# A decoder layer on one core: the split down weights of the first FFN go through DRAM between its two passes

## The chip, the cores and the metric

The kernel runs on one core of one Trainium2 chip. The metric is the time of one execution in microseconds (us) of device time; the median of three runs before the change is 1908.28 us.

## What is computed

One decoder layer over 1040 positions (16 meta tokens and 1024 inputs) of width 1024, in float32. Cut to what matters here:

```
h_res = h_res + 0.5 * swiglu_ffn(rmsnorm(h_res), w_gate, w_up, w_down)     # FFN 1, hidden width 2816
proj  = rmsnorm(h_res) @ w_in
h_res = h_res + concat([diff_attention(q, k, v), conformer_conv(u)]) @ w_out
h_res = h_res + 0.5 * swiglu_ffn(rmsnorm(h_res), w_gate2, w_up2, w_down2)  # FFN 2
y     = rmsnorm(h_res)[:, 16:]

swiglu_ffn(x, g, u, d) = (silu(x @ g) * (x @ u)) @ d
```

The down weights of FFN 1 are a 2816 x 1024 matrix; they are needed for every position.

## The kernel before

The positions are worked on in two halves, of 528 (the meta tokens with them) and of 512. So each FFN has two passes and reads all its weights twice. The hidden width is 22 blocks `f` of 128, in chunks of 4, 4, 4, 2, 4 and 4 blocks (`CHUNKS`). In a chunk TensorE first makes the gate and up products of its blocks (tiles `pg` and `pu`, or `p` where two blocks are made together by a scheme with seven products, class `Pairs`), VectorE and ScalarE turn them into the hidden activations `h`, and TensorE then makes the down products (`dn`): four weight tiles per chunk, each for two of the eight output blocks. VectorE adds each `dn` to the residual `x` (L241). Ahead of the down products of a chunk the next block or pair is already made (`pend`), except around the last chunk.

Products are made in fp32r, a reduced format, three times: each operand is split in a high part (`x` rounded) and a low part (the rest), and high by high, high by low and low by high are summed. Weights are split on the chip by `load_w` (L107 on): SyncE (SP) issues a load of 512 KB into a tile `wraw` (two slots), ScalarE (ACT) rounds it into the first half of a tile `whl` (L128), and VectorE (DVE) subtracts to make the second half (L129). `whl` has four slots, one rotation for all weights; a slot is free again when TensorE has read its tile to the end. `Pairs` has raw tiles of its own (`raw`) beside `wraw`. Each engine works through its instructions in program order, and so does the DMA queue of SP; that order is set by a scheduler, in which loads and splits of weights rank 500 places ahead (`AHEAD`).

In the second pass of FFN 1 the attention and the convolution of the first half run beside the FFN: attention scores `sc`, transposes `tm` and values `o` sit between the products of TensorE, and the 31-tap convolution (`acc`, L556) on VectorE. Both passes use the same down weights: in the first pass `ffn` is called with `FB[0]` (two blocks of 264 columns), in the second with `FB[1]` (one block of 512). GpSimd (POOL) issues only stores: `kscr`, `qscr`, `vscr` (keys, queries, values), `acscr`, `xscr` (the residual after a pass) and some small ones.

Of the kernel before, what the change touches and what calls it, by code (L numbers as in the profile page):

```python
# [9 lines left out]
F32 = mybir.dt.float32  # L10
F32R = mybir.dt.float32r
# [7 lines left out]
P = 128  # L19
# [7 lines left out]
CHUNKS = [4, 4, 4, 2, 4, 4]  # L27
PLAIN = 4
# [4 lines left out]
AHEAD = 500  # L33
# [7 lines left out]
FB = [[(0, HM // 2), (HM // 2, HM // 2)], [(0, HB)]]  # L41
# [10 lines left out]
def layer(ctx, tc, xb, wgu1, wd1, win, wv, wo, wgu2, wd2, colv, lamv, consts, cossin, out):  # L52
    nc = tc.nc
    V, S, T = nc.vector, nc.scalar, nc.tensor
    dma = nc.sync.dma_start
    store = nc.gpsimd.dma_start

    def mm(o, lhsT, rhs, start, stop):
        T.matmul(o, lhsT, rhs, start=start, stop=stop)  # L59

    def pool(stack, name, bufs, side="left"):
        return stack.enter_context(tc.tile_pool(name=name, bufs=bufs, side=side, reuse_waits="tile"))
# [3 lines left out]
    wph = pool(ctx, "whl", 4)  # L66
# [7 lines left out]
    dram = ctx.enter_context(tc.tile_pool(name="dscr", bufs=1, space=DRAM))  # L74
# [4 lines left out]
    xscr = dram.tile([2, P, ND, HB], F32, tag="xscr", name="xscr")  # L79
    rtok = dram.tile([2, HM], F32, tag="rtok", name="rtok")  # L80
    rscr = dram.tile([2, 4, HB], F32, tag="rscr", name="rscr")
    acscr = dram.tile([2, 8, P, 2, HB], F32, tag="acscr", name="acscr")

    rA = const.tile([P, HM], F32, tag="rA", name="rA")
# [13 lines left out]
    def col(i):  # L98
        return cols[:, i:i + 1]

    def psg(name):
        return psG.tile([P, 512], F32, tag="g", name=name)
# [4 lines left out]
    def load_w(src, n=1024, rp=None):  # L107
        with tc.high_priority(offset=AHEAD):
            raw = (rp or wpr).tile([P, 1024], F32, tag="wraw", name="wraw")
            dma(raw[:, :n], src)  # L110
            hl = wph.tile([P, 2, 1024], F32R, tag="whl", name="whl")
            split(hl[:, 0, :n], hl[:, 1, :n], raw[:, :n])
        return hl

    first = []
# [11 lines left out]
    def split(dst_hi, dst_lo, src):  # L127
        S.copy(dst_hi, src)  # L128
        return V.tensor_tensor(dst_lo, src, dst_hi.bitcast(F32), op=ALU.subtract)  # L129
# [43 lines left out]
    def tiles(hl, o=0, n=ND):  # L173
        return [hl[:, :, o + k * P:o + (k + 1) * P] for k in range(n)]
# [8 lines left out]
    def proj_pair(pss, hls, c0, w):  # L183
        for n, (a, xx) in enumerate(((0, xh), (1, xh), (0, xl))):
            for ps, hl in zip(pss, hls):
                for k in range(ND):
                    mm(ps, hl[:, a, k * P:(k + 1) * P], xx[:, k, c0:c0 + w], n == 0 and k == 0, n == 2 and k == ND - 1)

    def ffn(blocks, last_blocks, wgu, wd, x, after, step, before_last, start=False, scaled=False, flat=0, pair_of=None, ahead=None):
        def gate_up(f):  # L190
            if start and f < 2:
                hg, hu = first[2 * f:2 * f + 2]
            else:
                hg, hu = load_w(wgu[f, 0]), load_w(wgu[f, 1])
            if f >= flat:
                wsg, wsu = [tiles(hg, o, 4) + tiles(hu, o, 4) for o in (0, 512)]
            else:
                wsg, wsu = tiles(hg), tiles(hu)
            h = hp.tile([P, 2, HM], F32R, tag="h", name="h")
            for c0, w in blocks:  # L200
                pair = start and f == 0
                if pair:
                    if c0 == 0:
                        pg, pu = psg("pg")[:, :w], psg("pu")[:, :w]
                    else:
                        both = psS.tile([P, 2, 512], F32, tag="s", name="both")
                        pg, pu = both[:, 0, :w], both[:, 1, :w]
                    proj_pair((pg, pu), (hg, hu), c0, w)
                else:
                    pg = psg("pg")[:, :w]  # L210
                    proj(pg, wsg, c0, w)
                rb = rA[:, c0:c0 + w]
                tw = tmp.tile([P, 512], F32, tag="e", name="t")[:, :w]
                th = tmp.tile([P, 512], F32, tag="th", name="th")[:, :w]
                if scaled:
                    S.activation(th, pg, AF.Tanh, scale=0.5)
                    last[0] = V.scalar_tensor_tensor(tw, th, 1.0, pg, op0=ALU.add, op1=ALU.mult)  # L217
                else:
                    V.tensor_tensor(tw, pg, rb, op=ALU.mult)
                    S.activation(th, tw, AF.Tanh, scale=0.5)  # L220
                    V.tensor_tensor(tw, tw, rb, op=ALU.mult)
                    last[0] = V.scalar_tensor_tensor(tw, th, 1.0, tw, op0=ALU.add, op1=ALU.mult)
                step()
                if not pair:
                    pu = psg("pu")[:, :w]
                    proj(pu, wsu, c0, w)
                V.tensor_tensor(tw, pu, tw, op=ALU.mult)
                last[0] = split(h[:, 0, c0:c0 + w], h[:, 1, c0:c0 + w], tw)
            step()
            return [[h]]  # L230

        def down_piece(hl, n, j, d, hs, c0, w):
            m = psg("dn")
            for f in range(n):
                o = (j * n + f) * P
                wh, wl = hl[:, 0, o:o + P], hl[:, 1, o:o + P]
                mm(m[:, :w], wh, hs[f][0][:, 0, c0:c0 + w], f == 0, False)
                mm(m[:, :w], wh, hs[f][0][:, 1, c0:c0 + w], False, False)
                mm(m[:, :w], wl, hs[f][0][:, 0, c0:c0 + w], False, f == n - 1)
            xs = x[:, d, c0:c0 + w]  # L240
            last[0] = V.scalar_tensor_tensor(xs, m[:, :w], 0.25, xs, op0=ALU.mult, op1=ALU.add)  # L241

        def make(f):
            return pair_of(f) if pair_of and f >= flat else gate_up(f)

        offs = 0
        f = 0
        pend = []
        for ci, n in enumerate(CHUNKS):
            hs = pend  # L250
            final = ci == len(CHUNKS) - 1
            if final and ahead is not None:
                ahead()
            while len(hs) < n:
                new = make(f)
                f += len(new)
                hs = hs + new
            pend = []
            if final:
                if pair_of:  # L260
                    pair_of.flush()
                before_last()
            elif not (pair_of and f == flat):
                pend = make(f)
                f += len(pend)
            srcs = []
            for dp in range(4):
                sz = P * 2 * n * P
                srcs.append(wd[offs:offs + sz].rearrange("(p c) -> p c", p=P))
                offs += sz  # L270
            if not final:
                for dp in range(4):
                    hl = load_w(srcs[dp], 2 * n * P)
                    for j in range(2):
                        for c0, w in blocks:
                            down_piece(hl, n, j, 2 * dp + j, hs, c0, w)
                    step()
            else:
                hls = [load_w(s, 2 * n * P) for s in srcs]
                for c0, w in last_blocks:  # L280
                    for d in range(ND):
                        down_piece(hls[d // 2], n, d % 2, d, hs, c0, w)
                        after(c0, w, d)
# [63 lines left out]
    def mix_in(b, x):  # L347
        sums = {}

        def f(c0, w, d):  # L350
            if d == 0:
                sums[c0] = tmp.tile([P, 512], F32, tag="ssum", name="ssum")
            xs = x[:, d, c0:c0 + w]
            gain_piece(xs, col(C_GM + d), xh[:, d, c0:c0 + w], xl[:, d, c0:c0 + w])
            sq_piece(xs, w, sums[c0], d == 0)
            if d == ND - 1:
                norm_r(rB[:, c0:c0 + w], w, sums[c0], 95 if c0 + w == FB[b][-1][0] + FB[b][-1][1] else 60)
                a = max(c0, RO[b])
                store(xscr[b][:, :, a - RO[b]:c0 + w - RO[b]], x[:, :, a:c0 + w])
        return f  # L360
# [588 lines left out]
    x = ffn1_first()  # L949
# [4 lines left out]
    first_pairs = Pairs(wgu1, H2, {}, True)  # L954
# [46 lines left out]
        first_pairs.e = pool(es_s, "e1", 2, side="right")  # L1001

    first_pairs.ready.append(first_ready)
    ffn(FB[0], FB[0], wgu1, wd1, x, mix_in(0, x), first_step, setup_consts, start=True, flat=PLAIN, pair_of=first_pairs)
    es_s.close()
    es_z = ExitStack()
    zp.append(pool(es_z, "zp", 5, side="right"))
# [9 lines left out]
    x = res.pop()  # L1017
# [3 lines left out]
    bg = mixer(mid_pools(es_m, 0), zs)  # L1021
# [3 lines left out]
            pass  # L1025

    next(bg, None)
    ffn(FB[1], FB[1], wgu1, wd1, x, mix_in(1, x), lambda: next(bg, None), drain, scaled=True, flat=PLAIN)
    es_m.close()
    zs = []  # L1030
    es_l = ExitStack()
# [14 lines left out]
    x = res.pop()  # L1046
# [4 lines left out]
    bg = mixer(mid_pools(es_m, 1), zs)  # L1051
# [182 lines left out]
```

## Time and profile before

| what | value |
|---|---|
| median of 3 runs | 1908.28 us (1907.56 to 1909.43) |
| the profiled execution, its own time | 1906.57 us |
| its span, first to last instruction | 1904.8 us |
| TensorE busy, matmuls | 1883.7 us (99%) |
| TensorE weight loads (PEld) | 1673.5 us (88%) |
| VectorE busy | 1486.7 us (78%) |
| ScalarE busy | 828.5 us (43%) |
| read from HBM, written | 215.72 MB, 31.61 MB |

The profiled execution is one of the program, 1.71 us below the median of the three runs; 1.77 us of its time lie outside its span. In the span the first pass of FFN 1 has its down products and pairs from about 58 to 372 us, the input projection follows up to 497 us, and the second pass runs from 497 to 905 us. Shares of busy time are means over stages; which engine is waited for in a stage is read from the waits.

### The profile page before, as it was taken

How to read it: one execution, taken by the hardware profiler on the slowest of the kernel's cores; microseconds unless marked ns; L12 is line 12 of the kernel's file. 1: busy time of each engine (PE TensorE's matmuls, PEld its weight loads, DVE VectorE, ACT ScalarE, POOL GpSimd, SP SyncE). 2: the span in 40 equal slices, each digit the busy share in tenths (PEclk: the TensorE clock that was granted, in tenths of full speed). 3: DMA queues.
4: the chain of work that ended last, by engine and by line, in shares of the span. 5: the costliest groups of instructions: out<-in, count | busy, mean ns of one | idle time of the engine just before them, and what ended most of it. 6: DMA issues, size and time to landing. Idle time of an engine off the chain costs nothing.

```text
span 1904.8 us, 29083 instructions
## 1 busy us (share of the span) xinstructions
PE 1883.7 (99%) x11542; PEld 1673.5 (88%) x11542; DVE 1486.7 (78%) x2317; ACT 828.5 (43%) x1407; POOL 70.1 (4%) x132
## 2 busy tenths in 40 slices
PE   9999999999999999999999999999999999999997
PEld 9999999999888888778878888888879889999997
DVE  8997787867687877866558788888785898977877
ACT  6453444532333333534223354444453455434434
POOL 0000000003100000020001100000021000000000
PEclk9999999999999999999999999999999999999999
DMA  5232332445633333273535733424258533323322
GB/s 183 80 115 84 95 95 99 136 156 166 192 101 110 122 100 101 89 253 115 206 100 155 222 107 105 144 89 120 90 191 297 166 122 123 134 98 106 101 93 67
DMA packets 89000, 249.22 MB, mean 131 GB/s; under 512 B 10928, under 2 KB 26032, under 8 KB 88608
## 3 DMA queue, kind: packets, MB, share of 16 engines
q1 hardware_dynamic: 79888, 217.85, 35.6%
q0 software_dynamic: 8976, 29.52, 4.7%
q8 instruction: 90, 1.47, 0.3%
q14 instruction: 46, 0.38, 0.1%
HBM read 215.72 MB, written 31.61 MB: 130 GB/s over the span
## 4 chain that ended last, share of the span: by engine, by line
PE 89%; DVE 6%; DMA 2%; ACT 2%; issue 1%; SPq 0%; DVEq 0%; ACTq 0%
PE dn L59 24%; PE p L874 20%; PE pg L59 15%; PE pu L59 12%; PE pa L59 5%; PE pv L59 3%; PE pb L59 2%; PE wo L59 2%; PE sc L59 2%; DVE whl L129 2%; PE o L59 1%; ACT whl L128 1%; PE tm L482 1%; PE v L59 1%; DMA wraw<-wo 1%
## 5 line engine op out<-in xcount | busy, mean ns | idle before, releaser
L128 ACT CAST whl<-wraw 128x1024 fp32r<-128x1024 f32 (+1 forms) x317 | 324.9, 1025 | 471.6 <-PE dn L59 126.1
L59 PE MATMUL dn<-h,whl 128*128 128x512 f32 (+2 forms) x2736 | 508.8, 344 | 1.4 <-DVE x L241 0.5
L59 PEld LDWEIGHTS dn<-h,whl 128*128 128x128 f32 x2736 | 429.6, 188 | 65.7 <-ACT h L128 0.9
L129 DVE TENSOR_TENSOR whl<-wraw,whl 128x1024 fp32r<-128x1024 f32 (+1 forms) x317 | 378.0, 1192 | 126.3 <-ACT whl L128 124.2
L59 PE MATMUL pg<-xh,whl 128*128 128x512 f32 (+1 forms) x1008 | 300.3, 373 | 1.9 <-ACT xh L142 1.7
L59 PE MATMUL pu<-xh,whl 128*128 128x512 f32 (+1 forms) x816 | 251.4, 382 | 1.6 <-DVE t L217 1.6
L874 PE MATMUL p<-ext,whl 128*128 128x264 f32 (+1 forms) x1872 | 229.4, 282 | 0.0
L874 PEld LDWEIGHTS p<-ext,whl 128*128 128x128 f32 x1872 | 227.0, 188 | 0.5
L59 PEld LDWEIGHTS pg<-xh,whl 128*128 128x128 f32 x1008 | 183.7, 190 | 40.1 <-issue 4.7
L59 PE MATMUL pg<-xl,whl 128*128 128x512 f32 (+1 forms) x504 | 186.4, 372 | 0.7 <-DVE xl L129 0.7
L874 PE MATMUL p<-xh,whl 128*128 128x256 f32 (+1 forms) x992 | 182.1, 282 | 0.0
L556 DVE SCALAR_TENSOR_TENSOR acc<-z,cols,acc 128x512 f32<-128x512 f32 x240 | 179.3, 747 | 3.0
L59 PEld LDWEIGHTS pu<-xh,whl 128*128 128x128 f32 x816 | 150.2, 189 | 32.8 <-DVE t L217 2.0
L241 DVE SCALAR_TENSOR_TENSOR x<-dn,x 128x512 f32<-128x512 f32 (+2 forms) x248 | 137.9, 568 | 50.8 <-PE dn L59 50.3
L874 PEld LDWEIGHTS p<-xh,whl 128*128 128x128 f32 x992 | 154.5, 188 | 0.2 <-DVE eg L891 0.2
L59 PE MATMUL pu<-xl,whl 128*128 128x512 f32 (+1 forms) x408 | 154.5, 381 | 0.0
L874 PE MATMUL p<-xl,whl 128*128 128x256 f32 (+1 forms) x496 | 139.4, 281 | 0.0
L128 ACT CAST whl<-raw 128x1024 fp32r<-128x1024 f32 x80 | 84.0, 1050 | 117.7 <-PE p L874 46.5
L129 DVE TENSOR_TENSOR whl<-raw,whl 128x1024 fp32r<-128x1024 f32 x80 | 97.7, 1222 | 19.1 <-ACT whl L128 18.6
L59 PEld LDWEIGHTS pg<-xl,whl 128*128 128x128 f32 x504 | 94.9, 189 | 17.3 <-DVE xl L129 1.1
L874 PEld LDWEIGHTS p<-xl,whl 128*128 128x128 f32 x496 | 93.4, 188 | 0.0
L59 PE MATMUL pa<-xh,whl 128*128 128x264 f32 (+2 forms) x384 | 91.4, 323 | 0.0
(205 smaller groups left out, 2341.3 us busy)
## 6 DMA issues: line engine op xcount, KB each, us to landing
wraw<-wgu SPq DMA_DIRECT2D x135, 512.0 KB, 3.4
wraw<-wd SPq DMA_DIRECT2D x80, 512.0 KB, 3.4
raw<-wgu SPq DMA_DIRECT2D x40, 512.0 KB, 3.4
wraw<-win SPq DMA_DIRECT2D x32, 512.0 KB, 3.4
wraw<-wo SPq DMA_DIRECT2D x24, 512.0 KB, 4.3
q<-qscr SPq DMA_DIRECT2D x32, 256.0 KB, 5.4
acscr<-a POOLq DMA_DIRECT2D x32, 256.0 KB, 4.0
k<-kscr SPq DMA_DIRECT2D x8, 520.0 KB, 4.0
```

The source lines that it names most:

```text
L59: T.matmul(o, lhsT, rhs, start=start, stop=stop)
L128: S.copy(dst_hi, src)
L129: return V.tensor_tensor(dst_lo, src, dst_hi.bitcast(F32), op=ALU.subtract)
L241: last[0] = V.scalar_tensor_tensor(xs, m[:, :w], 0.25, xs, op0=ALU.mult, op1=ALU.add)
L482: T.transpose(tm[:, j], ps_[0][:, o:o + P], ident)
L556: V.scalar_tensor_tensor(a, z[:, j:j + HB], col(wc + j), a, op0=ALU.mult, op1=ALU.add)
L874: T.matmul(bank[mat], a, self.mov[m][b][k], start=first and k == 0 and i == 0 and (self.sep or mat == 0), stop=(self.sep or mat == 1) and ...
```

## The change

A new DRAM tensor `dnscr` holds the split down weights of FFN 1, both parts. In the first pass each down weight tile is loaded and split as before, and then stored by a DMA of GpSimd: 20 tiles of 1 MB and 4 of 512 KB (the chunk with two blocks). In the second pass the tile is loaded from `dnscr` straight into `whl` by one DMA of SP, with no `wraw` tile, no instruction of ScalarE and none of VectorE. FFN 2 is not changed.

```diff
+    dnscr = dram.tile([4 * len(CHUNKS), P, 2, 1024], F32, tag="dnscr", name="dnscr")
...
+    def load_dn(src, n, i, keep):
+        if keep != "load":
+            hl = load_w(src, n)
+            if keep:
+                store(dnscr[i, :, :, :n], hl[:, :, :n].bitcast(F32))
+            return hl
+        with tc.high_priority(offset=AHEAD):
+            hl = wph.tile([P, 2, 1024], F32R, tag="whl", name="whl")
+            dma(hl[:, :, :n].bitcast(F32), dnscr[i, :, :, :n])
+        return hl
...
             if not final:
                 for dp in range(4):
-                    hl = load_w(srcs[dp], 2 * n * P)
+                    hl = load_dn(srcs[dp], 2 * n * P, 4 * ci + dp, keep)
...
             else:
-                hls = [load_w(s, 2 * n * P) for s in srcs]
+                hls = [load_dn(s, 2 * n * P, 4 * ci + dp, keep) for dp, s in enumerate(srcs)]
...
-    ffn(FB[0], FB[0], wgu1, wd1, x, mix_in(0, x), first_step, setup_consts, start=True, flat=PLAIN, pair_of=first_pairs)
+    ffn(FB[0], FB[0], wgu1, wd1, x, mix_in(0, x), first_step, setup_consts, start=True, flat=PLAIN, pair_of=first_pairs, keep="store")
...
-    ffn(FB[1], FB[1], wgu1, wd1, x, mix_in(1, x), lambda: next(bg, None), drain, scaled=True, flat=PLAIN)
+    ffn(FB[1], FB[1], wgu1, wd1, x, mix_in(1, x), lambda: next(bg, None), drain, scaled=True, flat=PLAIN, keep="load")
```

How the order on the engines changes is seen at three places. The first is SP's queue in the second pass, ahead of the down products of the first chunk; `wd` are the down weights, `wgu` gate and up weights, `vt`, `k` and `q` the attention's operands. Before:

```order
L110 DMA wraw<-wgu 128x1024
L509 DMA vt<-vscr 128x4x256
L110 DMA wraw<-wgu 128x1024
L110 DMA wraw<-wd 128x1024 x4
L110 DMA wraw<-wgu 128x1024 x2
L415 DMA k<-kscr 128x528
L418 DMA q<-qscr 64x2x512
```

And of the change, whose line numbers are 12 higher in this part of the file:

```order
L111 DMA wraw<-wgu 128x1024
L521 DMA vt<-vscr 128x4x256
L111 DMA wraw<-wgu 128x1024 x3
L124 DMA whl<-dnscr 128x2048 x4
L427 DMA k<-kscr 128x528
L430 DMA q<-qscr 64x2x512
```

The four loads of 1 MB stand behind the two `wgu` loads that they stood ahead of, and still ahead of the keys and queries.

The second place is POOL's queue from its first DMA on; `dnscr` is stored in the first pass, `xscr` after its last down products. Before, and then with the change:

```order
L359 DMA xscr<-x 1024x1x248
L359 DMA xscr<-x 1024x1x264
L637 DMA rtok<-rB 16x1x33
```

```order
L120 DMA dnscr<-whl 128x2048 x12
L120 DMA dnscr<-whl 256x1x512 x4
L120 DMA dnscr<-whl 128x2048 x8
L371 DMA xscr<-x 1024x1x248
L371 DMA xscr<-x 1024x1x264
L649 DMA rtok<-rB 16x1x33
```

The 24 stores all come ahead of what was POOL's first DMA. On TensorE, ScalarE, VectorE and SP no instruction of the first pass moves.

The third place is ScalarE in the second pass at the same first chunk; `th` is the tanh of a gate, `p` and `pm` belong to the attention's softmax, `h` is the high part of the hidden activation. Before, and then with the change:

```order
L128 CAST whl<-wraw 128x1024
L216 ACTIVATE th<-pg 128x512
L456 ACTIVATE p,sm<-sc,nm 128x272
L471 ACTIVATE p<-p,sm 128x272
L128 CAST pm<-p 128x16
L475 CAST pm<-p 128x16
L128 CAST whl<-wraw 128x1024
L128 CAST h<-t 128x512
```

```order
L228 ACTIVATE th<-pg 128x512
L468 ACTIVATE p,sm<-sc,nm 128x272
L483 ACTIVATE p<-p,sm 128x272
L140 CAST pm<-p 128x16
L487 CAST pm<-p 128x16
L140 CAST h<-t 128x512
```

Only the roundings of down weights are gone; the rest stands in the same order.

## Rows read from the trace of the kernel before

**Rows 1.** The page: busy time and share of each engine.
```profile
PE 1883.7 (99%) x11542; PEld 1673.5 (88%) x11542; DVE 1486.7 (78%) x2317; ACT 828.5 (43%) x1407; POOL 70.1 (4%) x132
```

**Rows 2.** Busy time by window: first pass, projection, second pass of FFN 1.
```profile
core 0: us, PE busy (x) PEld busy (x) DVE busy (x) ACT busy (x) POOL busy (x), PEclk, DMA share, GB/s
60.00:370.00 310.00, 308.87 (x2527) 307.99 (x2526) 250.83 (x420) 146.63 (x258) 1.00 (x1) 1.00 0.31 99
497.00:905.00 408.00, 405.47 (x1848) 328.32 (x1847) 310.93 (x491) 166.10 (x315) 12.44 (x24) 1.00 0.41 131
```

**Rows 3.** All waits of TensorE, 497 to 905 us: total, times, longest.
```profile
PE sc L59 <- DMA q<-qscr: 2.4, 1, 2.4
PE tm L482 <- ACT p L456: 0.2, 1, 0.2
```

**Rows 4.** The chain that ended last, second pass: start us, us, what.
```profile
535.26 5.57 PE pg L59 x24
...
560.00 5.54 PE dn L59 x24
```

**Rows 5.** Groups by form, 497 to 905 us, ACT and DVE, whl alone.
```profile
L128 ACT CAST whl<-wraw 128x1024 fp32r<-128x1024 f32 x65 | 68.2, 1050 | 94.8 <-PE pu L59 53.6 <-PE dn L59 27.4 <-PE pg L59 13.5
L128 ACT CAST whl<-wraw 128x512 fp32r<-128x512 f32 x4 | 2.5, 622 | 7.2 <-PE pu L59 7.2
L129 DVE TENSOR_TENSOR whl<-wraw,whl 128x1024 fp32r<-128x1024 f32 x65 | 79.5, 1223 | 23.7 <-ACT whl L128 23.2
L129 DVE TENSOR_TENSOR whl<-wraw,whl 128x512 fp32r<-128x512 f32 x4 | 2.8, 690 | 1.0 <-ACT whl L128 1.0
```

**Rows 6.** DMA issues, whole run: count, KB each, median us to landing.
```profile
wraw<-wd SPq DMA_DIRECT2D x80, 512.0 KB, 3.4
wraw<-wo SPq DMA_DIRECT2D x24, 512.0 KB, 4.3
vt<-vscr SPq DMA_DIRECT2D x4, 1024.0 KB, 5.6
x<-xscr SPq DMA_DIRECT2D x2, 2048.0 KB, 10.2
xscr<-x POOLq DMA_DIRECT2D x1, 1056.0 KB, 5.2
```

**Rows 7.** Timeline, DVE and ACT, chunk of two blocks, first pass.
```profile
244.03 0.69 DVE L129 TENSOR_TENSOR whl<-wraw,whl 128x512 fp32r<-128x512 f32 x1 [1.29 <-ACT whl L128]
255.02 1.05 ACT L128 CAST whl<-wraw 128x1024 fp32r<-128x1024 f32 x1 [2.03 <-PE dn L59]
```

**Rows 8.** Timeline, end of the first pass: DVE, SP, ACT, PE.
```profile
344.91 1.23 DVE L129 TENSOR_TENSOR whl<-wraw,whl 128x1024 fp32r<-128x1024 f32 x1 [0.35 <-ACT whl L128]
343.23 3.26 SPq L110 DMA_DIRECT2D wraw<-wd  x2
350.04 1.05 ACT L128 CAST whl<-wraw 128x1024 fp32r<-128x1024 f32 x1 [0.21 <-DMA wraw<-wd]
353.07 0.41 ACT L128 CAST h<-t 128x264 fp32r<-128x264 f32 x1 [1.39 <-DVE t L899]
353.53 12.76 PE L59 MATMUL dn<-h,whl 128*128 128x264 f32 x103 [0.45 <-ACT h L128]
```

**Rows 9.** Timeline, POOL and DVE in the projection.
```profile
442.58 2.17 POOL L700 DMA_DIRECT2D kscr<-pk  x4 [0.52 <-DVE pk L129]
443.40 1.23 DVE L129 TENSOR_TENSOR whl<-wraw,whl 128x1024 fp32r<-128x1024 f32 x1
```

**Rows 10.** TensorE's wait at 512 us: timeline, then a window.
```profile
514.79 0.49 PE L59 MATMUL sc<-k,q 128*128 128x144 f32 x1 [2.35 <-DMA q<-qscr]
514.60:518.20 3.60, 3.41 (x10) 2.85 (x11) 0.31 (x1) 1.04 (x2) 0.00 (x0) 0.53 1.05 272
```

**Rows 11.** Timeline, PE, down products of the two-block chunk, second pass.
```profile
757.75 3.01 PE L59 MATMUL dn<-h,whl 128*128 128x512 f32 x12
...
764.82 4.57 PE L59 MATMUL dn<-h,whl 128*128 128x512 f32 x19
```

More of the change, by code (lines that the diff above doesn't have):

```diff
@@ L187, in proj_pair, with ffn @@
                     mm(ps, hl[:, a, k * P:(k + 1) * P], xx[:, k, c0:c0 + w], n == 0 and k == 0, n == 2 and k == ND - 1)
-    def ffn(blocks, last_blocks, wgu, wd, x, after, step, before_last, start=False, scaled=False, flat=0, pair_of=None, ahead=None):
+    def ffn(blocks, last_blocks, wgu, wd, x, after, step, before_last, start=False, scaled=False, flat=0, pair_of=None, ahead=None, keep=None):
         def gate_up(f):
```

## The prediction, before the change was run

> **What bounds the kernel now.** I read the page first, then busy time by stage, then TensorE's waits inside the stages that the change touches, then the chain, and last the timelines around the slots that the change holds longer or fills another way. The page shows TensorE at 99% of the span and VectorE at 78% [rows 1]. The reader is to see that this is no mean over stages with different limits: in the second pass of FFN 1, where the removed work lies, TensorE is busy 405.5 of 408 us, and in the first, where the stores are added, 308.9 of 310 [rows 2]. In the second pass TensorE waits twice in all, 2.4 us for a load of queries and 0.2 us for ScalarE, and never for a weight [rows 3]. Busy time of a matmul can hide a wait inside, so I look at the pace as well: a gate product of 24 matmuls of 512 columns takes 5.57 us and a down product of 24 takes 5.54 us [rows 4], 232 and 231 ns for each matmul. Gate weights come from `wraw` by ACT and DVE, down weights too, and neither holds TensorE up at the pace of one matmul behind the other.
>
> **What is removed.** In the second pass 24 splits of down weights go: of 1 MB tiles 20 x 1.050 = 21.0 us of ScalarE and 20 x 1.223 = 24.5 us of VectorE, and of the four half tiles 4 x 0.622 = 2.5 and 4 x 0.690 = 2.8 us [rows 5]. That is 23.5 us of ScalarE and 27.2 us of VectorE. ScalarE is busy 166.1 us of these 408 and VectorE 310.9 [rows 2], so both get emptier, but neither is what TensorE waits for. What the removal can return is at most what TensorE waits for them in this stage: 0.2 us [rows 3]. The wait for the queries is a DMA's and stands ahead of the first down product, where no queue is changed. I take -0.2 us, with 0 as the other bound.
>
> The order on TensorE is nearly untouched; in the fourth and fifth chunk a few score, transpose and value matmuls move by some places among the products. Each is one of attention's short waits at worst, and the longest of that kind in this stage is the 0.2 us above; I take 0.
>
> **What is moved in the second pass.** A down tile no longer waits in `wraw` for its slot; SP itself waits until TensorE has freed the slot, and then the load of 1 MB runs. Two things must hold. The first is time: the first down tile of a chunk takes the slot of a gate tile read four tiles earlier. In the first chunk that gate product ends at 535.26 + 5.57 = 540.8 us, the down products begin at 560.0 [rows 4], so 19.2 us are there, and the next tiles follow at a product's pace on both sides. The nearest load of this size takes 5.6 us (`vt`, 1 MB), and one of twice the size 10.2 us [rows 6]; both fit. The tightest place is the chunk with two blocks. Its last load is free to go when the down products begin at 757.75, and its tile is read after 36 of the 48 matmuls, ten matmuls into the row that begins at 764.82, so at about 767.1 [rows 11]: 9.4 us for 512 KB, which take 3.4 us, or 4.3 in a crowded stretch [rows 6]. The second is the queue: SP works in order, so while it waits for the fourth slot the keys and queries behind it wait too. That slot is free when the down products begin; the order shows that the two `wgu` loads have moved ahead of the four, and a key tile has only two slots, which are free when scores have read them, and those scores stand among the down products. Nothing on TensorE gets late; I take 0 here, with a bound of +0.8 us: if the load in the two-block chunk took the 10.2 us of one of 2 MB [rows 6], 10.2 - 9.4.
>
> **What is added in the first pass.** 20 stores of 1 MB and 4 of 512 KB. Nothing else of this pass moves on any engine. Three costs. (1) POOL issues them; its queue is empty there, 1.0 us busy in 310 [rows 2]. Whether its issuing slows VectorE is seen in the projection: a split beside four issues takes 1.23 us [rows 9], against a mean of 1.223 [rows 5]. I take 0. (2) A slot of `whl` is now free only when the store has read it too. The shortest hold is again the two-block chunk: the first tile is split at 244.03 + 0.69 = 244.7 and its slot is taken again at 255.0 [rows 7], 10.3 us later. The nearest store, of 1056 KB, lands in 5.2 us [rows 6], with up to 1 us for the issue 6.2. It is hidden with 4 us to spare, and where four blocks make a chunk the hold is longer. I take 0. (3) The stores share the DMA engines with the weight loads, and a load that is just in time comes late. In most of this pass such a delay has nowhere to go, since TensorE waits for nothing that a load feeds; but at its end there is one place without cover. ScalarE has the last down tile's rounding ahead of the rounding of `h`, for which TensorE waits 0.45 us; and that rounding of the weight already waits 0.21 us for its load, the second of the two that SP issues from 343.23 on (it starts at about 346.2 and lands at 350.0) [rows 8]. The store of the second down tile starts just then, at 344.91 + 1.23 = 346.1 [rows 8]. Every us that this load loses, ScalarE loses, `h` loses and TensorE loses. Bounds: nothing, if the DMA engines have room (they are busy 0.31 of the time in this pass, [rows 2]), and 5.2 us, if the whole store goes first [rows 6]. I take 0.9 us, which is what loads of 512 KB pay in the crowded stretch of `wo` over the usual ones, 4.3 - 3.4 [rows 6], since a load beside one store is nearer to that than to waiting a store out.
>
> On this the page "DMA: Bandwidth & Descriptors" of the Trainium skill, section "Issuing engines are not separate DMA queues", says that transfers from different engines run on the same 16 DMA engines and interleave; that POOL's queue is another than SP's is no shelter. It speaks against a cost of nothing; read as an even share it would double the 1.2 us that 512 KB take at that page's 435 GB/s (an estimate), +1.2 instead of +0.9, and the sum would be +1.0.
>
> **Sum.** -0.2 + 0.9 = +0.7 us. The profiled execution would go from 1906.57 to 1907.3 us; it stood 1.71 us under the median of the three runs, 1908.28, so for a median I take 1908.28 + 0.7 = 1909.0 us. Both terms are far inside about 0.2%, 3.8 us, which is about what a measurement of this kernel can tell from no change.
>
> **Rivals.** *Slower: the late load at the end of the first pass costs its upper bound.* This is mechanism (3) at its far end: the last down load waits behind a store. It decides the sign from a delay of 3.8 us on, and at 5.2 us gives 1908.28 + 5.2 - 0.2 = 1913.3 us. For it: this wait is the one place where ScalarE's order ties a load to TensorE directly. Against it: it needs the store to go first almost whole, and the DMA engines have two thirds of their time free. Chance 0.14.
>
> *Faster: waits hide in TensorE's busy time.* If the second pass ran at the pace of VectorE, 27.2 us less of it would give up to 27 us back, 1881 us. For it: weight loads fill only 328 of 408 us in this stage [rows 2]. Against it: the equal pace of 231 and 232 ns for weights that had just been split and for others, and 0.2 us of waits. Chance 0.03. The page "Perfetto Trace Analysis" of the Trainium skill, "Identifying the Most-Contended Engine", says that matmul busy share is no measure of what is left and that the share of weight loads is one; by it 20% of this stage would be open. The trace disagrees as far as waits go, by the rows named.
>
> *Faster: the wait for queries goes.* TensorE waits 2.35 us at 514.8 us, and the granted clock is 0.53 in the 3.6 us after it [rows 10], which costs about 1.7 us more; without both, 1908.28 - 4.1 + 0.7 = 1904.9, and a little more would do. For it: DMA timing alone decides it, and other stores come before it now. Against it: every queue involved is unchanged up to there. Chance 0.05.
>
> The forecast, within about 1 us of the sum and surely within 0.2%, has the remaining 0.78. Range: 1905.5 to 1912.5 us; the low end takes in the spread of the runs before and most of the lost wait, the high end a late load of 4 us. It leaves out the far parts of the rivals on both sides, some 0.15. From the same cases, with a fifth of the last rival's chance staying inside the bound: faster by over 0.2% 0.07, within 0.2% 0.79, slower 0.14.
>
> **What would show it.** In the profile of the changed kernel the second pass has 45 roundings and 45 splits of whole weight tiles, not 65, and no half ones; ScalarE and VectorE lose 23 and 27 us there, while TensorE's busy time in it stays within 2 us of 405, and its waits remain two. The 24 stores land in 4 to 7 us each, and no wait of ScalarE for a store appears. The last wait of ScalarE for a down load in the first pass grows from 0.21 to about 1 us and TensorE's wait for `h` from 0.45 to 1.3. HBM written goes from 31.6 to about 55 MB. I would be wrong if down products in the second pass wait for `dnscr` loads (SP held longer than the slots explain), if stores keep slots beyond 10 us, or if TensorE's second pass becomes shorter by more than 2 us.

## The result, and the profile after

The changed kernel is slower: 1924.25 us (median of four runs) against 1907.92 us, ratio 1.0083, 95% interval [1.0071, 1.0095]. In a second comparison it was 1919.16 against 1907.63 us, 1.0061 [1.0048, 1.0074]. Its profiled execution, the shortest of the four, took 1919.87 us (span 1918.1), 13.3 us over that of before; the medians are 16.3 us apart, so some 3 us of the loss stand in no row below. All traces below are single profiled executions; all ratios come from repeated runs beside the kernel before.

The page shows that the two engines that lost the splits are emptier, and nothing came of it (compare [rows 1]):

```profile
PE 1887.8 (98%) x11542; PEld 1675.2 (87%) x11542; DVE 1460.7 (76%) x2293; ACT 807.5 (42%) x1383; POOL 83.5 (4%) x156
```

In the windows of [rows 2] TensorE lost 6.3 us of busy time in the first pass and 2.1 us in the second:

```profile
60.00:370.00 310.00, 302.54 (x2452) 300.50 (x2451) 239.61 (x392) 139.23 (x241) 11.90 (x22) 0.99 0.46 162
497.00:905.00 408.00, 403.35 (x1876) 327.45 (x1875) 278.61 (x456) 140.40 (x285) 13.80 (x26) 0.99 0.47 160
```

All waits of TensorE in the changed kernel, 60 to 380 us and then 497 to 905 us (total, times, longest):

```profile
PE dn L59 <- DVE x L253: 4.2, 5, 1.4
PE dn L59 <- ACT h L140: 2.9, 1, 2.9
PE v L59 <- DVE ssum L149: 0.6, 1, 0.6
PE dn L59 <- DVE t L239: 0.2, 1, 0.2
```

```profile
PE v L59 <- ACT sq L540: 3.3, 1, 3.3
PE sc L59 <- DMA q<-qscr: 1.4, 1, 1.4
```

The same view of the kernel before, 60 to 370 us (its second pass is [rows 3]):

```profile
PE dn L59 <- DVE x L241: 0.5, 1, 0.5
PE dn L59 <- ACT h L128: 0.5, 1, 0.5
PE dn L59 <- DVE t L227: 0.2, 1, 0.2
```

No wait in these stretches names a weight or a store. TensorE waits for evacuations (`x`), for `h` and for sums, all of them the work of VectorE and ScalarE. What holds those two up is seen one step further back. First the landing times in the first pass, 100 to 375 us, changed kernel, then before (count, KB each, median us to landing; compare [rows 6]):

```profile
dnscr<-whl POOLq DMA_DIRECT2D x16, 1024.0 KB, 8.3
wraw<-wd SPq DMA_DIRECT2D x16, 512.0 KB, 4.1
wraw<-wgu SPq DMA_DIRECT2D x14, 512.0 KB, 5.3
```

```profile
wraw<-wd SPq DMA_DIRECT2D x16, 512.0 KB, 3.4
wraw<-wgu SPq DMA_DIRECT2D x14, 512.0 KB, 3.3
```

Now one place in the middle of the pass, the begin of the third chunk's down products. Timeline of the changed kernel (SP, POOL, ACT, DVE, PE):

```profile
203.09 3.50 SPq L111 DMA_DIRECT2D wraw<-wd  x2
209.78 5.11 SPq L849 DMA_DIRECT2D wraw<-wgu  x2
203.35 0.53 POOL L120 DMA_DIRECT2D dnscr<-whl  x1 [53.91 <-DVE whl L141]
206.52 0.53 POOL L120 DMA_DIRECT2D dnscr<-whl  x1 [2.64 <-DVE whl L141]
210.05 0.53 POOL L120 DMA_DIRECT2D dnscr<-whl  x1 [2.99 <-DVE whl L141]
214.83 0.53 POOL L120 DMA_DIRECT2D dnscr<-whl  x1 [4.25 <-DVE whl L141]
207.44 1.05 ACT L140 CAST whl<-wraw 128x1024 fp32r<-128x1024 f32 x1 [2.70 <-DMA wraw<-wd]
212.23 1.05 ACT L140 CAST whl<-wraw 128x1024 fp32r<-128x1024 f32 x1 [1.67 <-DMA wraw<-wd]
217.73 1.23 DVE L860 TENSOR_TENSOR raw<-raw,wraw 128x1024 f32<-128x1024 f32 x1 [2.51 <-DMA wraw<-wgu]
218.87 0.77 DVE L253 SCALAR_TENSOR_TENSOR x<-dn,x 128x264 f32<-128x264 f32 x2
219.35 14.77 PE L59 MATMUL dn<-h,whl 128*128 128x264 f32 x120 [1.23 <-DVE x L253]
```

And the same loads and roundings before:

```profile
202.03 3.55 SPq L110 DMA_DIRECT2D wraw<-wd  x2
207.87 3.59 SPq L837 DMA_DIRECT2D wraw<-wgu  x2
205.53 1.05 ACT L128 CAST whl<-wraw 128x1024 fp32r<-128x1024 f32 x1 [1.84 <-PE p L874]
208.79 1.05 ACT L128 CAST whl<-wraw 128x1024 fp32r<-128x1024 f32 x1
```

The reader is to see the coincidence: a split lets go a `wraw` slot and a finished tile in the same instant, so SP's next load (203.09) and POOL's store (203.35) start together, again and again: 22 of the 24 stores start 0.27 us behind a load. And the stores come some 3 us apart and take 8.3 us each, so the next one starts while the last is still under way. ScalarE then waits 2.70 and 1.67 us for raw weights, where before it waited for no load at this place. VectorE waits 2.51 us for a raw gate tile, and behind that one instruction in its queue stand two evacuations that had no need of it; TensorE waits 1.23 us for the first of them, which frees the accumulator that its next product needs. Busy share of the DMA engines over this place, before and after:

```profile
201.00:217.00 16.00, 16.00 (x134) 16.00 (x133) 13.97 (x24) 6.66 (x12) 0.00 (x0) 1.00 0.48 152
```

```profile
203.00:219.00 16.00, 15.12 (x125) 14.92 (x124) 9.31 (x16) 6.22 (x10) 2.12 (x4) 1.00 0.92 356
```

At the end of the pass the place that the prediction named is the dearest one (timeline of ACT, PE; compare [rows 8]). ScalarE waits 2.57 and 1.94 us for the last two loads, `h` stands behind them, and TensorE waits 2.90 us:

```profile
353.30 1.05 ACT L140 CAST whl<-wraw 128x1024 fp32r<-128x1024 f32 x1 [2.57 <-DMA wraw<-wd]
358.35 1.05 ACT L140 CAST whl<-wraw 128x1024 fp32r<-128x1024 f32 x1 [1.94 <-DMA wraw<-wd]
361.84 14.35 PE L59 MATMUL dn<-h,whl 128*128 128x264 f32 x103 [2.90 <-ACT h L140]
```

Right behind it, by the window, its granted clock is 0.51, the lower level, for 3.5 us:

```profile
362.50:366.00 3.50, 3.50 (x18) 3.50 (x17) 2.27 (x6) 2.20 (x7) 0.00 (x0) 0.51 1.02 383
```

In the second pass there is one place, in the fifth chunk (SP, POOL, ACT, PE):

```profile
816.27 3.11 SPq L124 DMA_DIRECT2D whl<-dnscr  x2
816.27 0.54 POOL L557 DMA_DIRECT2D acscr<-a  x1 [304.84 <-ACT a L140]
822.89 0.62 ACT L140 CAST a<-acc 128x512 fp32r<-128x512 f32 x1 [4.97 <-DMA acscr<-a]
824.62 1.91 PE L59 MATMUL v<-sq,onesH 128*32 128x512 f32 x2 [3.25 <-ACT sq L540]
```

The window behind that wait:

```profile
823.40:830.40 7.00, 5.79 (x9) 1.67 (x10) 1.88 (x4) 2.72 (x6) 1.08 (x2) 0.52 0.40 164
```

One ready tile of 1 MB is loaded in the instant at which POOL stores 256 KB of attention's output, and a second one 2.8 us later, at 819.05 (the row above takes both together). `a` has two slots of the tag `rs`, one for its high and one for its low part, so the next rounding of `a` must wait until that store has landed and starts 6.6 us after its issue; `sq` stands behind it on ScalarE and TensorE's `v` behind `sq`. Before, the store and the next rounding were (POOL, ACT):

```profile
808.44 0.54 POOL L545 DMA_DIRECT2D acscr<-a  x1 [307.47 <-ACT a L128]
810.94 0.62 ACT L128 CAST a<-acc 128x512 fp32r<-128x512 f32 x1
```

The sum by these rows: waits in the first pass 7.9 - 1.2 = +6.7 us; the clock there 3.5 x (1 - 0.51) = +1.7; waits in the second pass 4.7 - 2.6 = +2.1; the clock there, on 5.79 us of busy time, 5.79 x (1 - 0.52) = +2.8; and the fall after the query wait [rows 10], 3.41 x (1 - 0.53) = 1.6, did not come this time. That is +11.7 of 13.3 us; the last 1.6 us are not assigned to rows. At least 0.5 us have nothing to do with the stores: the first down weights are loaded at 35.14 us instead of 34.62, before any store, and the granted clock of the first 20 us is 0.83 instead of 0.91.

Matched one by one in the two traces, the evacuations of `x` show where the first pass loses its time: nothing in the first chunk, 0.6, 1.5, 2.2 and 1.1 us in the next four, and 5.6 in the last, 10.9 us in all (the waits and the clock above name 8.4 of them). About 3 us come back at the query wait.

### The profile page after: what moved, and what is told of

The parts are those of the page before. It is cut to its first block, busy times and chain, and to the rows that moved or that the text cites. A ratio compares the mean times of both kernels' runs of the same rounds, so it can differ in the third digit from the quotient of the medians.

```text
span 1918.1 us, 29045 instructions
## 1 busy us (share of the span) xinstructions
PE 1887.8 (98%) x11542; PEld 1675.2 (87%) x11542; DVE 1460.7 (76%) x2293; ACT 807.5 (42%) x1383; POOL 83.5 (4%) x156
## 4 chain that ended last, share of the span: by engine, by line
PE 71%; issue 17%; DVE 5%; DMA 4%; ACT 1%; POOL 0%; SPq 0%; DVEq 0%; ACTq 0%; POOLq 0%
PE p L886 19%; PE dn L59 18%; PE pg L59 10%; PE pu L59 7%; PE pa L59 5%; PE wo L59 4%; PE pb L59 2%; DMA wraw<-wgu 2%; PE pv L59 2%; PE sc L59 2%; DVE whl L141 1%; PE o L59 1%; DMA wraw<-wd 1%; PE v L59 1%; ACT whl L140 1%
## 5 line engine op out<-in xcount | busy, mean ns | idle before, releaser
L140 ACT CAST whl<-wraw 128x1024 fp32r<-128x1024 f32 (+1 forms) x293 | 301.5, 1029 | 445.0 <-PE dn L59 110.6
L141 DVE TENSOR_TENSOR whl<-wraw,whl 128x1024 fp32r<-128x1024 f32 (+1 forms) x293 | 350.3, 1195 | 120.9 <-ACT whl L140 117.3
```

## The experiments

The theory (T): the 23 MB of stores and the larger loads make other transfers late at a few places, and the in-order ScalarE and VectorE carry each delay to TensorE. Against it stood the slots of `whl` held by the stores (H), the issuing on GpSimd (I), mere bytes (B), and a loss that lies in one pass alone (R).

**One half of the change each.** The first kernel has the stores alone:

```
-... scaled=True, flat=PLAIN, keep="load")
+... scaled=True, flat=PLAIN)
```

> The first pass stores all 24 down tiles as the changed kernel does, the second pass loads and splits raw weights as before. Theory T (the stores' traffic makes just-in-time weight loads late, and the in-order ScalarE and VectorE carry the delay to TensorE): the first pass ends about 10 us later, as in the changed kernel, so with the wait for the queries kept or lost the time is 1915 to 1919 us; TensorE busy in 60:370 near 303 of 310, several VectorE waits of 1 to 2.6 us for raw gate or pair weights. Rival R (the loss lies in the second pass's new loads, and the first pass only shows noise): within 2 us of the kernel before, 1906 to 1910 us.

1914.07 us, 1.0044 [1.0031, 1.0057], a microsecond below T and far from R; TensorE is busy 302.88 of the 310 us, with six waits for `x` (4.3 us) and one for `h` (2.8). By the evacuations of `x` the first pass loses 10.0 us in this trace, 5.3 of them in the last chunk, without any fall of the clock; 2.6 us come back at the query wait, which is shorter here (1.9 us) and has no fall behind it. The second kernel has the loads alone, all 24 from the one tile that is stored:

```
-            if keep:
+            if keep and i == 0:
...
-            dma(hl[:, :, :n].bitcast(F32), dnscr[i, :, :, :n])
+            dma(hl[:, :, :n].bitcast(F32), dnscr[0, :, :, :n])
```

> No stores but one: only the first down tile is stored, and the second pass loads that one tile 24 times in place of the 24 (its weights are so not those of the reference). Theory T: the first pass is as before, within 1 us. In the second pass the loads of 1 MB on SP may meet the stores of acscr: if that is tied to these loads, ScalarE waits 2 to 5 us for an acscr store, TensorE 2 to 3 us at the v of the fifth chunk and its clock falls for 7 us: 1911 to 1914 us. If it needs the shift of the first pass, the time is 1906 to 1909 us. Rival R (all of the loss is from these loads): 1919 us or more.

1912.38 us, 1.0027 [1.0016, 1.0038]: the collision is tied to the loads and needs no shift from the first pass. Its waits, ACT and PE, 497 to 905 us:

```profile
ACT a L140 <- DMA acscr<-a: 7.0, 3, 4.9
PE v L59 <- ACT sq L540: 3.1, 1, 3.1
```

R falls both ways, and 0.44 + 0.27 = 0.71% lies between the two measurements of the whole change (0.61 and 0.83%). That one was run again beside other kernels:

> The changed kernel itself, beside the others. If its loss is the sum of the two found alone (7.0 us by the stores, 5.3 us by the loads): 1919.5 to 1921 us. If they add to each other (a second acscr wait, the clock): 1923 to 1926 us, as in the comparison.

1919.16 us, as told above; just under the plain sum of the two; the first comparison gave the larger value. The two measurements of one kernel differ by 0.22%, about a third of the effect, and no run shows why. So whether the two losses add to each other stays open; the sum of their ratios does not need it.

**The stores: bytes, slots or issue?** In this group the second pass loads raw weights, as in the first experiment. Thin stores keep the issue and leave out seven eighths of the bytes:

```
-store(dnscr[i, :, :, :n], hl[:, :, :n].bitcast(F32))
+store(dnscr[i, :, :, :n // 8], hl[:, :, n - n // 8:n].bitcast(F32))
```

> Stores only, as in the first experiment, but each of the 24 writes an eighth of its columns (2.9 MB in all in place of 23.1); issue on GpSimd, its waits and the hold on the weight slot are kept, only shorter in time. Theory T (traffic): the loss is a fraction of that of the stores at full size, 1907 to 1910 us. Rival I (the issuing on GpSimd, or the wait on whl's splitting, costs): as the stores at full size, 1915 to 1919 us.

1905.00 us, 0.9992 [0.9983, 1.0001]: no loss, and TensorE's waits from 60 to 380 us are those of before, so issuing on GpSimd costs nothing (24 issues, 0.69 us each in this trace). I falls. Next the full bytes from a tile that is no weight slot:

```
+copy = cpy[0]
+nc.gpsimd.tensor_copy(copy[:, n - 1:n], hl[:, 1, n - 1:n].bitcast(F32))
+for a in range(2):
+    store(dnscr[i, :, a, :n], copy[:, :n])
```

> Stores only, with the full 23.1 MB, but from a tile of its own that a GpSimd copy of one column releases when the down tile is split; the weight slots are not held by a store. (onesH is placed later, to make room; DRAM gets other data.) Theory T (traffic): the loss is that of the stores at full size, 1914 to 1919 us, with the same late loads. Rival H (the slots of whl, held longer by the stores, delay the next splits): 1907 to 1910 us.

1911.79 us, 1.0023 [1.0013, 1.0034], about half of the loss, between both expectations. The wait for `h` at the end is there as before (2.7 us) without any slot held, so H does not explain that one. But the run is muddled: with one `copy` tile GpSimd waited 12 times, 59.7 us in all, for its own earlier stores, so many of them started later than in the changed kernel. That suggested the next kernel, in which SP issues the stores; in SP's order each then stands behind the loads of the next weights:

```
-store(dnscr[i, :, :, :n], hl[:, :, :n].bitcast(F32))
+dma(dnscr[i, :, :, :n], hl[:, :, :n].bitcast(F32))
```

> The stores alone, all 24 and all their bytes, but issued by SP: in its order each stands behind one to three loads of the next weights, so a store starts when those loads are under way. Theory T (what costs is that a store starts at the same instant as the load that its tile's split has let go): the waits for x go and the loss is small, 1907 to 1910 us. Rival B (23 MB more on the DMA engines cost their time anyhow): as from GpSimd, 1912 to 1916 us. Rival Q (SP, waiting for a split ahead of a store, holds the loads behind it): over 1916 us.

1909.10 us, 1.0003 [0.9994, 1.0012]: the same bytes from the same slots, and no measurable loss. Timeline around the place shown above (SP, DVE, PE):

```profile
205.78 0.33 SPq L111 DMA_DIRECT2D wraw<-wd  x1
209.38 0.33 SPq L849 DMA_DIRECT2D wraw<-wgu  x1
209.76 0.42 SPq L120 DMA_DIRECT2D dnscr<-whl  x1
204.54 1.22 DVE L141 TENSOR_TENSOR whl<-wraw,whl 128x1024 fp32r<-128x1024 f32 x1
213.95 1.22 DVE L860 TENSOR_TENSOR raw<-raw,wraw 128x1024 f32<-128x1024 f32 x1
208.84 13.33 PE L59 MATMUL dn<-h,whl 128*128 128x264 f32 x109
```

The tile split at 204.54 is stored at 209.76, 4.0 us after its split's end, when two further loads are issued; in the changed kernel the store followed its split by 0.3 us. VectorE no longer waits for the gate tile and TensorE runs through. The slots are held longer than ever here, so H falls for good, and so do B and Q. The waits did not all go, against T's words: `x` 4.3 to 2.3 us, `h` 2.8 to 0.9.

T is not shown in its own words either: 18 of the 24 stores still start 0.38 us behind a load, and other loads are still late (the one of 205.78 lands in 5.9 us, as its counterpart does in the changed kernel). What differs is which load is late. The gate load that VectorE had waited for, of 209.78 in the changed kernel and of 209.38 here, lands in (KB, us)

```profile
wraw<-wgu SPq DMA_DIRECT2D x1, 512.0 KB, 7.9
```

```profile
wraw<-wgu SPq DMA_DIRECT2D x1, 512.0 KB, 4.1
```

While it was under way, three stores ran beside it in the changed kernel and one here. So the cost of a store lies in which load it runs beside, and with how many others; the issuing and the slot do not set it, and the bytes alone do not. This run moved the stores to a later place and into the loads' own queue at once. That the queue is not needed is seen in the run with the other tile: there GpSimd's stores, held back by the one tile, never have more than 1 MB under way, the loads land in 3.6 and 4.1 us where the changed kernel has 4.1 and 5.3, and by the evacuations the first five chunks together lose 0.1 us; what is lost there is lost in the last chunk (3.5 us).

Leaving out the last chunk's four stores shows how uneven the cost is:

```
-            if keep:
+            if keep and i < 20:
```

> The stores alone, without those of the last chunk's four tiles (20 stores, 19 MB). Theory T (each loss belongs to one late load): the wait for h at the end of the first pass falls from 2.8 back to about 0.5 us and the one for ssum goes, the five short waits for x stay (4 us): 1909.5 to 1912 us. Rival (a loss spread over the pass by the bytes): a sixth less than with all stores, 1913 us.

1911.28 us, 1.0014 [1.0005, 1.0023]. Without a sixth of the stores 0.30 of the 0.44% is gone; the wait for `h` is 0.7 us and the one for `ssum` gone. By the evacuations of `x` the last chunk loses 0.2 us instead of 5.3. Not all of the 0.30% is the last chunk's: the chunks before it lose 2.5 us here and 4.7 with all stores, though their stores are the same (waits for `x` 2.0 and 4.3 us), so this part varies from one execution to the next.

**The loads: which collision?** First the fifth chunk's tiles are loaded raw and split again, the other twenty ready:

```
-        if keep != "load":
+        if keep != "load" or 16 <= i < 20:
```

> As the loads alone (one tile stored, its ready form loaded in the second pass), but the four tiles of the fifth chunk are loaded raw and split as before. Theory T2 (the 5 us of the loads alone are one collision: whl loads of that chunk beside the store of acscr): no wait of TensorE for sq at the v of the fifth chunk, no fall of the clock there, 1905 to 1909 us. Rival (the loads cost at many places a little, or the collision moves to another chunk): 1910 to 1913 us.

1907.76 us, 0.9999 [0.9990, 1.0008]; TensorE's only wait in the pass is the one for queries, 1.7 us. So the whole loss of the loads comes from this chunk. But three things came back together: smaller loads, the moment at which they start (a raw load waits for a slot of `wraw`, a ready one for a slot of `whl`), and a rounding that stood on ScalarE between `a` and `a` (the second of the two stands behind). Therefore half the bytes without the roundings, in the fifth chunk alone (the low parts are left out, VectorE writes zeros there):

```
+            if 16 <= i < 20:
+                dma(hl[:, 0, :n].bitcast(F32), dnscr[0, :, 0, :n])
+                V.memset(hl[:, 1, :n].bitcast(F32), 0.0)
```

> As the loads alone, but in the fifth chunk only the high half of each ready tile is loaded (512 KB, as raw weights had) and VectorE fills the low half with zeros, so ScalarE's roundings are gone there and the traffic is the old one (the low parts of these weights are left out). Theory T2a (the bytes of the ready load delay the acscr store): ScalarE's wait for the store falls from 4.9 us to below 2, TensorE's wait of 3.1 us at the v to below 1, and the clock stays: 1906 to 1909 us. Rival T2b (the roundings that are gone had spaced ScalarE's queue, and the wait comes from their absence): 1911 to 1914 us with the wait kept.

1908.68 us, 1.0005 [0.9997, 1.0014]. The time goes as T2a said, the rows only part of the way (ACT, PE; then the landing of the store that ScalarE waits for: KB, us):

```profile
ACT a L144 <- DMA acscr<-a: 5.8, 2, 3.5
PE v L59 <- ACT sq L544: 1.5, 1, 1.5
acscr<-a POOLq DMA_DIRECT2D x1, 256.0 KB, 5.1
```

And the window around that wait, at 814.6 us:

```profile
814.00:823.40 9.40, 8.80 (x33) 5.62 (x34) 6.25 (x11) 4.59 (x9) 1.08 (x2) 1.00 0.20 75
```

The longest wait for the store falls from 4.9 to 3.5 us, that of TensorE from 3.1 to 1.5, and the clock stays at its upper level. The store lands in 5.1 us; beside the loads of 1 MB in the changed kernel it took 6.5, and in the kernel before 2.3:

```profile
acscr<-a POOLq DMA_DIRECT2D x1, 256.0 KB, 2.3
```

So half the bytes give back a third of the delay. The missing rounding had taken 1.05 us and explains about 1 us of the wait that is left. The rest is the moment: in the kernel before, the raw loads of this chunk are issued up to 800.3 us and again from 811.6 us on, none near the store at 808.44; the ready load waits for a `whl` slot that a `pu` product frees, and is issued with the store (808.24 and 808.25 us here, 816.27 and 816.27 in the changed kernel). That the moment alone would do it is argued from these rows; no run moves a ready load and nothing else. What the run saves besides the 1.6 us of TensorE's wait is the fall of the clock.

**Remedies, alone and together.** The whole change with its stores on SP:

```
-store(dnscr[i, :, :, :n], hl[:, :, :n].bitcast(F32))
+dma(dnscr[i, :, :, :n], hl[:, :, :n].bitcast(F32))
```

> The changed kernel with its stores issued by SP and nothing else altered. Theory T: only the loss of the second pass is left, 1912 to 1915 us, the wait at the v of the fifth chunk as in the loads alone. Rival (the two losses are not independent, the second needs the first): 1907 to 1910 us.

1913.77 us, 1.0031 [1.0021, 1.0041], with 3.3 us of wait at `v`: the loss of the loads alone. The whole change without the fifth chunk (stores on GpSimd):

```
-        if keep != "load":
+        if keep != "load" or 16 <= i < 20:
...
-            if keep:
+            if keep == "store" and not 16 <= i < 20:
```

> The changed kernel with its stores on GpSimd, but the fifth chunk's four tiles neither stored nor loaded ready. Theory T: the loss of the stores is left, less the fifth chunk's waits (1 to 1.5 us): 1911 to 1914 us; no acscr wait above 2 us. Rival (the second loss moves to another chunk): 1917 us or more.

1915.07 us, 1.0038 [1.0024, 1.0052]: the wait at `v` is gone and the loss of the stores stays, 1 us above T, whose waits for `x` fell only to 3.3 us. Both of these edits together:

> The changed kernel with both remedies: the stores are issued by SP behind the loads of the next tiles, and the fifth chunk's tiles are neither stored nor loaded ready. Theory T: both losses are gone, and since TensorE bounds both passes nothing is won either: 1905 to 1910 us. Rival (bytes cost, wherever they stand): 1914 us or more.

1908.24 us, 1.0000 [0.9991, 1.0009]. Both losses are gone, twenty of the 24 splits are still saved, and nothing is won.

## Why the prediction was wrong, step by step

It forecast 1909.0 us and a range up to 1912.5; the kernel took 1924.25.

- **What is removed: right.** 24 roundings and 24 splits fewer (ACT x1407 to x1383, DVE x2317 to x2293), worth nothing that can be measured: with the collisions taken out and 20 of the 24 splits still saved the ratio is 1.0000 [0.9991, 1.0009]. The rival of waits hidden in TensorE's busy time is refuted by the same run.
- **Stores, (1) issue and (2) slots: right.** Thin stores and stores on SP cost nothing measurable, and no wait of TensorE, VectorE or ScalarE in the first pass names one of these stores. The size in (2) was too small, though: a store of 1 MB took 8.3 us, not 5.2, and the forecast landing of 4 to 7 us did not come.
- **Stores, (3) the DMA engines: the step that failed.** "In most of this pass such a delay has nowhere to go, since TensorE waits for nothing that a load feeds" was read from TensorE's waits alone. The loads feed ScalarE and VectorE, and behind a late load in their queues stand evacuations and `h`, for which TensorE has little slack. A wait list of TensorE before the change cannot show that; the trace could have, by naming for each raw load what stands behind its reader and how long before it is needed. In place of one delay of 0.9 us the changed kernel's trace showed about 6.7 us of waits at seven places plus a fall of the clock, by the evacuations 10.9 us over the pass; the stores alone cost 0.44%. At the end of the pass, the one place that was named, `h` went from 0.45 to 2.90 us, inside the bound of 5.2, but with what followed the last chunk lost 5.6. The size for a load beside one store was right: the load of 203.09 took 4.3 us, 0.9 over the usual 3.4. The sum had left out that the stores overlap: the next two loads took 5.9 and 7.9 us.
- The mean DMA share of 0.31 [rows 2] was no evidence of room. The stores do not start at random but at the instants when loads start; over the 16 us shown the share went from 0.48 to 0.92. On this the prediction named a page of the Trainium skill, "DMA: Bandwidth & Descriptors", section "Issuing engines are not separate DMA queues": the traces agree that transfers of another engine share the DMA engines, 3.4 and 3.3 us of landing becoming 4.1 and 5.3. Its estimate of +1.2 us for one load was of the right size (+0.7 and +2.0); the number of loads that count was wrong.
- **Loads in the second pass, taken as 0: failed.** They were in time for TensorE, as worked out; no product waits for `dnscr`. The prediction saw that SP would wait for TensorE to free a slot, and asked only whether the tile would be in time; what it left out is what else starts in that instant. From the store of `acscr` to the next rounding of `a` 6.6 us went by, where before it was 2.5, and the removal of a rounding brought that next rounding forward by about 1 us. That is 0.27%, more than the bound of +0.8 us, and the sign "no wait of ScalarE for a store appears" was not kept (5.0 us).
- **The clock** entered the prediction only where it stood already [rows 10]. By the profiled rows its new falls are 1.7 + 2.8 = 4.5 us of the loss, less the 1.6 us of the one after the query wait. Whether the latter comes differs between executions of the same kernel: the profile of the repeated run has a query wait of 3.2 us and a fall behind it. So the rival of the query wait came in this one execution, hidden under a larger loss.
- The slower rival had the right sign and the right kind of mechanism, but one place; it would have given 1913.3 us.

## What to carry to other kernels

Before adding or moving a transfer, list the transfers that will be under way beside it and, for each, what stands behind its reader on an in-order engine; TensorE's own list of waits, and a mean DMA share, hide this. A store that has no hurry can be issued behind the loads that have: from their queue the same bytes cost nothing measurable here. A transfer that waits for another slot also starts at another moment, and meets other transfers there. Taking work off an engine that is not the bound wins nothing, and may bring an instruction forward into a wait that the work had covered.

## What was not expected of the hardware

A store of 1 MB by GpSimd beside loads took 8.3 us (median) where one of 1056 KB had taken 5.2, so the stores were slowed as well as the loads; a store of 256 KB went from 2.3 to 6.5 us beside loads of 1 MB. A wait of TensorE of 2.90 us was followed by 3.5 us at a granted clock of 0.51 and one of 3.25 us by 7.0 us at 0.52; after one of 1.5 us it stayed at 1.00. The length of the wait alone does not decide it: at the end of the first pass it stayed at 1.00 after waits of 2.63, 2.67 and 2.77 us in three runs (the change without the fifth chunk, the repeat, the stores alone), and fell after one of 2.66 us in the run with the other tile. The wait of 3.25 us and the fall behind it cost 3.25 + 2.8 = 6.1 us together; in the run with half the bytes, where the wait was 1.5 us and no fall followed, nearly all of the loss was gone.
